# Attention's combine step and the closing output stage of a hybrid decoder layer: longer-lived buffers, two DMA queues, norm weights in PSUM, residual on GpSimd

## The chip, the cores and the metric

The kernel runs on one core of a Trainium2 chip. The core has TensorE (PE, matrix products into PSUM), VectorE (DVE), ScalarE (ACT), GpSimd (POOL) and SyncE (SP, which here only starts DMA transfers), an on-chip memory SBUF and the matrix result memory PSUM with eight banks. Each engine works through its own instruction list strictly in order; a waiting instruction holds up everything behind it on its engine. The metric is the device time of one execution in microseconds (us), less is better: the median of three runs.

## What is computed

One layer of a decoder trunk with four parallel token mixers over 2048 tokens of width 1024, all in float32. What this change touches is the end of mixer A (an attention of four heads of 64 channels, with three dilations whose outputs are weighted by their softmax denominators) and everything behind it:

```
outs, lses = [], []
for window, dil in DILATED_PAIRS:              # three branches
    o, lse = _dilated_branch(q, k, v, window, dil, slopes)
    outs.append(o); lses.append(lse)
w = jax.nn.softmax(jnp.stack(lses), axis=0)    # weights of the branches
ya = jnp.einsum('gbhs,gbhsd->bhsd', w, jnp.stack(outs))
...
y = jnp.concatenate([ya * silu(ag), yb * silu(bg), yc * silu(cg), yd * silu(dg)], axis=-1)
y = jnp.einsum('bse,ed->bsd', y, w_out)        # 1024 x 1024 output projection
return x + _rms_norm(y, post_g)                # residual + normalised projection
```

## The kernel before

**Stages.** The input projection and mixers B, C and D come first (lines 143 to 536); their gated outputs go to memory (`yb_d`). Attention follows in two passes, `attention(0)` for heads 0 and 1 and `attention(1)` for heads 2 and 3. The last stage is the output projection with norm and residual (`final`, line 820), one tile of 128 tokens at a time, 16 tiles. A float32 product is made of three: each operand is split into a rounded "high" part and a "low" remainder, and high*high, high*low and low*high are added up in PSUM. That is why so many places have a copy that makes the high part and a subtraction that makes the low part.

**Order of the work.** The program is written as a dependence graph; a planner, which plays the program on a cost model, fixes each engine's list before anything runs, and earlier program text has priority. The order on each engine is therefore fixed, but the lines of the source do not give it one to one.

**From attention's statistics to the combine.** For each head and dilation `keep_stats` (line 719) writes maxima and denominators to memory (`st_d`). When a head is done, `weigh` (line 737) loads them (line 740, tile `sv`), works out the three branch weights per token on DVE and ACT (lines 741 to 752) and stores them (line 753, `f_d`). `combine` (line 755) then works on a pair of heads, chunk by chunk of tokens: two DMAs (line 763) read the weights of the two heads back, each broadcast over 64 partitions, into `fb` (128 x 3 x chunk); a third (line 765) loads the gate `sga`; POOL multiplies two branches by their weights (lines 766 and 767), DVE the third and adds the three (768 to 770) and applies the gate (772); ACT and DVE or POOL split the result into high and low (776, 777), tile `ysa`. For heads 0 and 1 chunks are 256 tokens with two buffers each for `fb` and `sga`, taken from pool `p2`, and the result goes to memory (`ya_d`, line 779) and comes back for the last stage (tile `ya0`, line 878). For heads 2 and 3 chunks are 512 tokens with two buffers each from pool `p4`, which is opened only after attention's pools `pm` and `p2` are closed, and the result is kept in SBUF. `weigh` and `combine` issue their DMAs on SP. Groups of 512 tokens are taken in the order 2, 3, 0, 1.

**Partials.** For the first 9 token tiles the six non-attention blocks of the projection are done while attention runs: `partial` (line 813) fills PE's gaps, and stores its sum in `part_d` (line 818). `issue_after` ties each partial to a point of the attention. The weights of the output projection are loaded and split by `out_weights` (line 543); blocks 1 to 3 come between the two attention passes, block 0 (the attention channels) after the last partial (line 868).

**The last stage.** Tiles 9 to 15 are "full" (48 matmuls of 128x512 each), tiles 0 to 8 "have" a partial (12 matmuls). `order` starts with the full tiles 9, 10 and 11, then runs three or two have tiles ahead of each full one and ends with full tile 15. A full tile loads its non-attention blocks (`yraw`) and splits them (`split_y`, lines 788 to 800: high part on ACT, low part on DVE). PE sums each 512-wide half in a PSUM bank (tag `fin`, 8 banks). A have tile adds the loaded partial on DVE (836); a full tile is copied by ACT (838). ACT squares and sums (844, for the last tile 840); DVE runs a ten-instruction chain for the inverse root (845, 124 to 135); then DVE multiplies by the root and the norm weights `post_b` (849), adds the residual (850), and SP stores the tile (851). Tile `z4` has 4 buffers, each held from the load of the partial, or from ACT's copy, until the store has landed.

```
for ns in halves if last else [slice(0, DM)]:
    V.scalar_tensor_tensor(z[:, ns], z[:, ns], rstd, post_b[:, ns], ALU.mult, ALU.mult)
    V.tensor_tensor(z[:, ns], z[:, ns], xr[:, ns], ALU.add)
    D.dma_start(out[0, t * P:(t + 1) * P, ns], z[:, ns])
```

Here V is DVE, A is ACT, G is POOL and D is SP.

Of the kernel before, what the change touches and what calls it, by code (L numbers as in the profile page):

```python
# [9 lines left out]
F32 = mybir.dt.float32  # L10
# [4 lines left out]
ALU = mybir.AluOpType  # L15
# [19 lines left out]
SLOPES = tuple(2.0 ** -(2 * (h + 1)) for h in range(4))  # L35
T_1, T_4, T_16, T_HEAD = 0, 256, 512, 640
MASKED = 1e30
PB = {"part": 1, "fin": 8}
N_S, N_T, N_O = 2, 3, 2
CORD = (2, 3, 0, 1)  # L40
CB0, B_PR, B_PT = 2, 6, 3

# [43 lines left out]
def hymba(ctx: ExitStack, tc: tile.TileContext, x, pre_g, w_in, sgu_g, sgu_w, sgu_b, pool_w,  # L86
# [4 lines left out]
    def r32(ap):  # L91
        return ap.bitcast(F32)
# [462 lines left out]
    def attention(p, tab):  # L555
        o01 = (big if p == 0 else po).tile([P, 2, SEQ], F32, tag="big" if p == 0 else "o01", name="att_o01")
        o = [o01[:, 0], o01[:, 1], po.tile([P, SEQ], F32, tag="o2", name="att_o2")]
        for s in range(2):
# [11 lines left out]
            for b, dil in enumerate(DILS):  # L570
# [22 lines left out]
                st = p2.tile([P, 2, 16], F32, tag="stat", bufs=2, name="att_st")  # L593
                branch(h, dil, qb, k2a, k2b, vt, tab, o[b], st)
                keep_stats(h, b, dil, st)
            weigh(h)
        return o

    def branch(h, dil, q2, k2a, k2b, vt, tab, o, st):
# [134 lines left out]
            else:  # L734
                D.dma_start(dst.rearrange("(w r i) -> r w i", r=16, i=8), src.rearrange("r (w i) -> r w i", i=8))

    def weigh(h):

        sv = p2.tile([P, 3, 2, 16], F32, tag="sv", bufs=2, name="sv")
        D.dma_start(sv.rearrange("q b z f -> q (b z) f"), st_d[h].rearrange("b z (q f) -> q (b z) f", f=16))  # L740
# [12 lines left out]
        D.dma_start(f_d[h].rearrange("b (q f) -> q b f", f=16), ew)  # L753

    def combine(p, o, pool, bufs, keep, step, order):

        kept = {}
        nb = step // P
        for c0 in order:
            cs = slice(c0, c0 + step)  # L760
            fb = pool.tile([P, 3, step], F32, tag="fb", bufs=bufs, name="fb")
            for s in range(2):
                D.dma_start(fb[s * HD:(s + 1) * HD], f_d[2 * p + s][:, cs].partition_broadcast(HD))
            sg = pool.tile([P, step], F32, tag="sga", bufs=bufs, name="sga")
            D.dma_start(sg, ag_d[p][:, cs])
            G.tensor_tensor(fb[:, 1], fb[:, 1], o[1][:, cs], ALU.mult)
            G.tensor_tensor(fb[:, 2], fb[:, 2], o[2][:, cs], ALU.mult)
            V.tensor_tensor(fb[:, 0], fb[:, 0], o[0][:, cs], ALU.mult)
            V.tensor_tensor(fb[:, 0], fb[:, 0], fb[:, 1], ALU.add)
# [5 lines left out]
            ys = pool.tile([P, 2, step], F32R, tag="ysa", bufs=4 if keep else CB0, name="ysa")  # L775
            A.activation(ys[:, 0], y, AF.Copy)
            (V if keep else G).tensor_tensor(ys[:, 1], y, r32(ys[:, 0]), ALU.subtract)
            if not keep:
                D.dma_start(ya_d[c0 // GRP][:, :, c0 % GRP:c0 % GRP + step], r32(ys))
            kept[c0 // step] = ys  # L780
        return kept

    def load_y(t, pool):
# [4 lines left out]
    def split_y(raw, pool, eng):  # L788

        ys = []  # L790
        for e in range(0, 6, 3):
            yt = pool.tile([P, 3, 2, P], F32R, tag="yt", bufs=2, name="yt")
            src = raw[:, e:e + 3]
            if eng is A:
                A.activation(yt[:, :, 0], src, AF.Copy)
            else:
                eng.tensor_copy(yt[:, :, 0], src)
            (V if eng is A else G).tensor_tensor(yt[:, :, 1], src, r32(yt[:, :, 0]), ALU.subtract)  # L798
            ys += [yt[:, j] for j in range(3)]
        return ys  # L800

# [11 lines left out]
    def partial(t):  # L813
        z = p3.tile([P, DM], F32, tag="z", bufs=2, name="z")
        ys = split_y(load_y(t, p3), p3, G)
        for n in range(2):
            A.activation(z[:, n * GRP:(n + 1) * GRP], out_proj(ys, range(2, 8), n, ps2, "part"), AF.Copy)
        D.dma_start(part_d[t * P:(t + 1) * P], z)

    def final(t, have, yb, py, p4, ps4, post_b, last):  # L820
# [24 lines left out]
        V.tensor_scalar(ss[:, :1], ss[:, :1], 1.0 / DM, EPS, ALU.mult, ALU.add)  # L845
        rstd = small.tile([P, 16], F32, tag="rstd", name="rstd2")[:, :1]
        rsqrt(rstd, ss[:, :1], 1)
        for ns in halves if last else [slice(0, DM)]:
            V.scalar_tensor_tensor(z[:, ns], z[:, ns], rstd, post_b[:, ns], ALU.mult, ALU.mult)
            V.tensor_tensor(z[:, ns], z[:, ns], xr[:, ns], ALU.add)  # L850
            D.dma_start(out[0, t * P:(t + 1) * P, ns], z[:, ns])
# [19 lines left out]
    ps4 = ctx.enter_context(tc.tile_pool(name="ps4", bufs=8, space=PSUM, reuse_waits="tile"))  # L871
    full, have = list(range(npart, SEQ // P)), list(range(npart))
    early = {t: load_y(t, p3 if i < 2 else p4) for i, t in enumerate(full[:3])}
    post_b = p4.tile([P, DM], F32, name="post_b")
    ya = [[p4.tile([P, 2, GRP], F32R, tag="ya0", bufs=4, name="ya0") for g in range(NG)]]
    ya.append(combine(1, o, p4, 2, True, GRP, [c * GRP for c in CORD]))
    for g in CORD:
        D.dma_start(r32(ya[0][g]), ya_d[g])
# [35 lines left out]
```

## Time and profile before

| what | us |
|---|---|
| median of three runs | 1062.74 (1060.38 to 1069.5) |
| the profiled execution, its own time | 1066.84 |
| span of its instructions | 1065.1 |
| PE busy | 993.5 (93% of the span) |
| DVE busy | 540.4 (51%) |
| ACT busy | 379.6 (36%) |
| POOL busy | 190.9 (18%) |

The profile counts time from the first instruction of the span. A "busy" engine executes an instruction; issuing a DMA does not count. A view of the timeline has start, duration, engine, source line, operation, output and inputs, and in brackets how long the engine had been idle and what it then waited for. The granted clock is TensorE's share of its full speed. The columns of the table by stages are named in its header. Matmuls overlap, so that their starts, and not their durations, tell PE's pace.

### The profile page before, as it was taken

Reading aid. Unit: us, or ns where it says so; the run is one execution under the profiler, and the core shown is the slowest. Engines: PE = TensorE matmul, PEld = TensorE weight load, DVE = VectorE, ACT = ScalarE, POOL = GpSimd, SP = SyncE. Lnnn points to the kernel's source line nnn. Section 1 sums busy time; section 2 is a strip of 40 time slices with the busy share of each in tenths; the row PEclk is TensorE's granted clock in tenths of the full one; section 3 lists DMA queues with packets and bytes.
Section 4 is the critical chain, followed back from the end, with each engine's and each line's share of the span. In section 5 each row is a group of like instructions: output and inputs, shape, how many; then the busy total and the mean of one; then the engine's idle time right before and its main releaser. Section 6 shows DMA issues by size and latency. Waiting matters only on the chain. (4 is left out here: it accounts for less than half of the span.)

```text
span 1065.1 us, 15690 instructions
## 1 busy us (share of the span) xinstructions
PE 993.5 (93%) x5916; PEld 855.0 (80%) x5916; DVE 540.4 (51%) x1547; ACT 379.6 (36%) x851; POOL 190.9 (18%) x195
## 2 busy tenths in 40 slices
PE   5899999999999999999999999979998779988993
PEld 5888898988877988989898787778988569867872
DVE  7611216696332422023763321287776677547898
ACT  6320222131222421122211121498877448513231
POOL 2310012211232000002210134031122351142000
PEclk9999999999999999999999999998999879989997
DMA  8530313233223331042211830395659953484776
GB/s 279 147 99 20 100 60 114 85 120 92 86 79 99 99 100 39 25 135 80 80 41 50 210 119 20 116 213 162 147 168 201 207 152 85 109 270 129 268 259 217
DMA packets 119962, 135.27 MB, mean 127 GB/s; under 512 B 14928, under 2 KB 95952, under 8 KB 117840
## 3 DMA queue, kind: packets, MB, share of 16 engines
q1 hardware_dynamic: 119888, 134.29, 43.6%
q8 instruction: 46, 0.75, 0.3%
q14 instruction: 28, 0.23, 0.1%
HBM read 97.80 MB, written 36.47 MB: 126 GB/s over the span
## 5 line engine op out<-in xcount | busy, mean ns | idle before, releaser
L95 PE MATMUL ps_t<-hh,w 128*128 128x512 f32 x1152 | 370.1, 398 | 2.3 <-DVE b_t L370 2.3
L95 PEld LDWEIGHTS ps_t<-hh,w 128*128 128x128 f32 x1152 | 216.7, 189 | 52.4 <-issue 3.4
L95 PE MATMUL ps_t<-hl,w 128*128 128x512 f32 x576 | 227.6, 395 | 0.0
L95 PE MATMUL ps_m<-w,hh 128*128 128x256 f32 x1024 | 183.8, 282 | 2.0 <-ACT hh L230 1.6
L95 PE MATMUL ps_out<-wo,yt 128*128 128x512 f32 x576 | 155.6, 414 | 6.1 <-DVE yt L798 3.1
L95 PEld LDWEIGHTS ps_m<-w,hh 128*128 128x128 f32 x1024 | 157.5, 190 | 3.9 <-ACT hh L230 2.8
L95 PE MATMUL ps_m<-w,hl 128*128 128x256 f32 x512 | 145.4, 284 | 0.2 <-DVE hl L231 0.2
L95 PEld LDWEIGHTS ps_out<-wo,yt 128*128 128x128 f32 x576 | 109.8, 198 | 31.1 <-DVE yt L798 4.4
L95 PEld LDWEIGHTS ps_t<-hl,w 128*128 128x128 f32 x576 | 108.7, 189 | 24.3 <-issue 1.4
L250 DVE TENSOR_TENSOR w<-raw,w 128x1024 fp32r<-128x1024 f32 x42 | 59.0, 1412 | 109.6 <-ACT w L248 109.4
L95 PEld LDWEIGHTS ps_m<-w,hl 128*128 128x128 f32 x512 | 97.6, 191 | 0.8 <-DVE hl L231 0.4
L641 ACT ACTIVATE att_p<-att_p,att_st 128x128 f32<-128x128 f32 (+1 forms) x192 | 86.4, 453 | 20.5 <-DVE att_st L639 20.0
L248 ACT ACTIVATE w<-raw 128x1024 fp32r<-128x1024 f32 (+1 forms) x56 | 55.0, 997 | 70.1 <-PE ps_t L95 37.6
L639 DVE CUSTOM_DVE_ANT_0 att_p<-ps_s,tab 128x128 f32<-128x128 f32 (+1 forms) x192 | 60.3, 357 | 34.5 <-PE ps_s L95 31.0
L95 PE MATMUL ps_o<-pt_hi,att_v 128*128 128x128 f32 (+1 forms) x204 | 54.4, 287 | 6.2 <-DVE att_o L664 4.2
L649 DVE TENSOR_TENSOR pt_lo<-ps_pt,pt_hi 128x512 fp32r<-128x512 f32 x80 | 51.2, 650 | 12.5 <-ACT pt_hi L648 12.1
L95 PE MATMUL ps_o<-pt_lo,att_v 128*128 128x128 f32 (+1 forms) x204 | 52.8, 294 | 3.5 <-DVE pt_lo L649 3.4
L98 PE MATMUL ps_pt<-ident,att_p 128*128 128x128 f32 x300 | 51.2, 283 | 0.8 <-ACT att_p L641 0.8
L95 PEld LDWEIGHTS ps_o<-pt_hi,att_v 128*128 128x128 f32 x204 | 40.8, 200 | 9.5 <-DVE att_o L664 4.6
L648 ACT ACTIVATE pt_hi<-ps_pt 128x512 fp32r<-128x512 f32 x80 | 44.1, 563 | 11.2 <-PE ps_pt L98 5.7
L95 PE MATMUL ps_s<-k2a,q2b 128*128 128x128 f32 (+1 forms) x128 | 37.5, 325 | 8.6 <-DMA k2a<-qk 4.4
L95 PEld LDWEIGHTS ps_o<-pt_lo,att_v 128*128 128x128 f32 x204 | 40.6, 199 | 5.9 <-DVE pt_lo L649 4.8
(160 smaller groups left out, 1319.8 us busy)
## 6 DMA issues: line engine op xcount, KB each, us to landing
raw<-in_w_in_dram SPq DMA_DIRECT2D x52, 512.0 KB
qk<-qk_s SPq DMA_DIRECT2D x16, 512.0 KB
att_v<-vd SPq DMA_DIRECT2D x8, 1024.0 KB
xr<-in_x_dram SPq DMA_DIRECT2D x16, 512.0 KB
out_dram<-z SPq DMA_DIRECT2D x15, 512.0 KB
xt<-in_x_dram SPq DMA_DIRECT2D x7, 1024.0 KB
yraw<-yb SPq DMA_DIRECT2D x16, 384.0 KB
partd<-z SPq DMA_DIRECT2D x9, 512.0 KB
```

Of the source, the lines that this page charges most:

```text
L95: return T.matmul(o, lhsT, rhs, start=start, stop=stop, skip_group_check=True)
L98: T.transpose(o, i, ident[:n, :n])
L248: A.activation(hi, raw[:, :, cs], AF.Copy, scale=sc)
L250: eng.tensor_tensor(lo, raw[:, :, cs], r32(hi), ALU.subtract)
L639: V.tensor_tensor_reduce(out=pr[:, u, :w], in0=ps[:, u, :w], in1=bb, scale=-SLOPES[h] * HD ** -0.5, scalar=3e38, op0=ALU.add, op1=ALU.min, ...
L641: A.activation(pr[:, u, :w], pr[:, u, :w], AF.Exp, bias=neg, scale=-1.0, accum_out=st[:, 1, n:n + 1])
L648: A.activation(hi, pt[:, :w], AF.Copy)
L649: V.tensor_tensor(lo, pt[:, :w], r32(hi), ALU.subtract)
```

## The change

- `combine` takes `fb` and `sga` from a new pool `pc`, opened ahead of attention's pools and kept to the end. Chunks are 256 tokens for both pairs of heads, two buffers each. The result of heads 2 and 3 is written into tiles of 512 tokens, half by half.
- In `combine` the first head's broadcast and the gate come first, then the second head's broadcast; the latter goes on ACT's DMA queue for heads 2 and 3, as do the load and the store in `weigh` for head 3.
- `post_b` moves to PSUM: the norm weights are loaded into a buffer of tag `z4` and copied by two ACT instructions into a tile of two banks; the banks for projection sums go from 8 to 6.
- Line 849's multiplication is done in halves of 512 for all tiles; the residual (line 850) goes to POOL for all tiles but the last.
- `split_y` makes the low parts on POOL everywhere.
- `out_weights(0)` comes ahead of the last two partials.

```
-PB = {"part": 1, "fin": 8}
+PB = {"part": 1, "fin": 6}
+N_FB = 2
...
-            weigh(h)
+            weigh(h, A if h == 3 else D)
...
-    def weigh(h):
+    def weigh(h, q):
-        D.dma_start(sv..., st_d[h]...)
+        q.dma_start(sv..., st_d[h]...)
-        D.dma_start(f_d[h]..., ew)
-    def combine(p, o, pool, bufs, keep, step, order):
+        q.dma_start(f_d[h]..., ew)
+    def combine(p, o, pool, keep, order):
-        nb = step // P
+        step, nb = 256, 2
+        q = A if keep else D
-            fb = pool.tile([P, 3, step], F32, tag="fb", bufs=bufs, name="fb")
-            for s in range(2):
-                D.dma_start(fb[s * HD:(s + 1) * HD], f_d[2 * p + s][:, cs].partition_broadcast(HD))
-            sg = pool.tile([P, step], F32, tag="sga", bufs=bufs, name="sga")
+            fb = pc.tile([P, 3, step], F32, tag="fb", bufs=N_FB, name="fb")
+            sg = pc.tile([P, step], F32, tag="sga", bufs=N_FB, name="sga")
+            D.dma_start(fb[:HD], f_d[2 * p][:, cs].partition_broadcast(HD))
             D.dma_start(sg, ag_d[p][:, cs])
+            q.dma_start(fb[HD:], f_d[2 * p + 1][:, cs].partition_broadcast(HD))
...
+                    kept[g] = pool.tile([P, 2, GRP], F32R, tag="ysa", bufs=4, name="ysa")
+                ys = kept[g][:, :, part]
...
-            (V if eng is A else G).tensor_tensor(yt[:, :, 1], src, r32(yt[:, :, 0]), ALU.subtract)
+            G.tensor_tensor(yt[:, :, 1], src, r32(yt[:, :, 0]), ALU.subtract)
...
+        for ns in halves:
+            V.scalar_tensor_tensor(z[:, ns], z[:, ns], rstd, post_b[:, ns], ALU.mult, ALU.mult)
         for ns in halves if last else [slice(0, DM)]:
-            V.scalar_tensor_tensor(z[:, ns], z[:, ns], rstd, post_b[:, ns], ALU.mult, ALU.mult)
-            V.tensor_tensor(z[:, ns], z[:, ns], xr[:, ns], ALU.add)
+            (V if last else G).tensor_tensor(z[:, ns], z[:, ns], xr[:, ns], ALU.add)
...
+    pc = ctx.enter_context(tc.tile_pool(name="pc", bufs=1, side="right", reuse_waits="tile"))
...
-        combine(0, o, p2, 2, False, 256, range(0, SEQ, 256))
+        combine(0, o, p2, False, range(0, SEQ, 256))
...
+                if t == npart - 2:
+                    out_weights(0, G)
                 partial(t)
-        out_weights(0, G)
...
-    post_b = p4.tile([P, DM], F32, name="post_b")
+    post_s = p4.tile([P, DM], F32, tag="z4", bufs=4, name="post_s")
+    post_b = ps4.tile([P, DM], F32, tag="gain", bufs=1, name="post_b")
-    ya.append(combine(1, o, p4, 2, True, GRP, [c * GRP for c in CORD]))
+    ya.append(combine(1, o, p4, True, [c * GRP + z for c in CORD for z in (0, 256)]))
-    D.dma_start(post_b, post_g[0].partition_broadcast(P))
+    D.dma_start(post_s, post_g[0].partition_broadcast(P))
+    for n in range(2):
+        A.activation(post_b[:, ns], post_s[:, ns], AF.Copy)      # ns: half n
```

More of the change, by code (lines that the diff above doesn't have):

```diff
@@ L774, in combine @@
                             sg.rearrange("p (n r i) -> p n r i", n=nb, r=16), ALU.mult)
-            ys = pool.tile([P, 2, step], F32R, tag="ysa", bufs=4 if keep else CB0, name="ysa")
+            g, part = c0 // GRP, slice(c0 % GRP, c0 % GRP + step)
+            if keep:
+                if g not in kept:
+                    kept[g] = pool.tile([P, 2, GRP], F32R, tag="ysa", bufs=4, name="ysa")
+                ys = kept[g][:, :, part]
+            else:
+                ys = pool.tile([P, 2, step], F32R, tag="ysa", bufs=CB0, name="ysa")
             A.activation(ys[:, 0], y, AF.Copy)
@@ L778, in combine @@
             if not keep:
-                D.dma_start(ya_d[c0 // GRP][:, :, c0 % GRP:c0 % GRP + step], r32(ys))
-            kept[c0 // step] = ys
+                D.dma_start(ya_d[g][:, :, part], r32(ys))
         return kept
@@ L866, in hymba @@
             with tc.issue_after(marks[int(len(marks) * (t + spread[0]) / npart * spread[1])]):
+                if t == npart - 2:
+                    out_weights(0, G)
                 partial(t)
[L868 removed]
     p4 = ctx.enter_context(tc.tile_pool(name="p4", bufs=1, reuse_waits="tile"))
[L871 removed]
+    ps4 = ctx.enter_context(tc.tile_pool(name="ps4", bufs=6, space=PSUM, reuse_waits="tile"))
     full, have = list(range(npart, SEQ // P)), list(range(npart))
     early = {t: load_y(t, p3 if i < 2 else p4) for i, t in enumerate(full[:3])}
[L874 removed]
+    post_s = p4.tile([P, DM], F32, tag="z4", bufs=4, name="post_s")
+    post_b = ps4.tile([P, DM], F32, tag="gain", bufs=1, name="post_b")
     ya = [[p4.tile([P, 2, GRP], F32R, tag="ya0", bufs=4, name="ya0") for g in range(NG)]]
[L876 removed]
+    ya.append(combine(1, o, p4, True, [c * GRP + z for c in CORD for z in (0, 256)]))
     for g in CORD:
         D.dma_start(r32(ya[0][g]), ya_d[g])
[L879 removed]
+    D.dma_start(post_s, post_g[0].partition_broadcast(P))
+    for n in range(2):
+        ns = slice(n * GRP, (n + 1) * GRP)
+        A.activation(post_b[:, ns], post_s[:, ns], AF.Copy)
     order = full[:3]
```

4 lines of the change are left out of this document (2 added, 2 removed).

## Prediction

> **What bounds the kernel now.** I first read the table by stages (start:end and length of the stretch, then busy us and instruction count of PE, PEld, DVE, ACT and POOL, then PE's granted clock, DMA share, GB/s).
>
> ```profile
> 800.00:880.00 80.00, 64.71 (x354) 54.67 (x353) 54.04 (x166) 42.24 (x136) 30.83 (x37) 0.85 0.81 187
> 880.00:925.00 45.00, 44.80 (x315) 41.19 (x314) 30.77 (x102) 35.38 (x104) 6.07 (x8) 0.99 0.29 67
> 925.00:985.00 60.00, 52.35 (x209) 40.69 (x208) 34.47 (x57) 15.45 (x30) 17.88 (x10) 0.94 0.70 207
> 985.00:1047.00 62.00, 60.28 (x261) 48.49 (x259) 53.79 (x161) 18.06 (x34) 0.00 (x0) 1.00 0.78 268
> 1047.00:1066.00 19.00, 0.00 (x0) 0.00 (x0) 14.72 (x40) 3.56 (x8) 0.00 (x0) 0.61 0.47 171
> ```
>
> Until 925 PE works on attention and partials. From 800 to 880, beside the first combine, it loses 15.3 us idle and a good part of its clock. From 925 on the second combine and the last stage run: PE loses 7.7 us by 985, little until 1047, and then the core runs 18 us without a matmul, with DVE busy nearly throughout. These two losses are where the change works. PE's own timeline, its idle gaps in brackets:
>
> ```profile
> 933.27 0.73 PE L95 MATMUL ps_out<-wo,yt 128*128 128x512 f32 x2 [1.16 <-ACT yt L795]
> 935.70 10.55 PE L95 MATMUL ps_out<-wo,yt 128*128 128x512 f32 x32 [1.71 <-DVE yt L798]
> ...
> 959.77 2.11 PE L95 MATMUL ps_out<-wo,ysa 128*128 128x512 f32 x8 [2.05 <-ACT ysa L776]
> ...
> 977.34 0.51 PE L95 MATMUL ps_out<-wo,ysa 128*128 128x512 f32 x1 [1.48 <-DVE ysa L777]
> ...
> 1041.05 4.28 PE L95 MATMUL ps_out<-wo,yt 128*128 128x512 f32 x18
> 1045.17 0.85 PE L95 MATMUL ps_out<-wo,ya 128*128 128x512 f32 x3
> 1045.85 0.85 PE L95 MATMUL ps_out<-wo,ysa 128*128 128x512 f32 x3
> ```
>
> At full clock 18 matmuls take 1045.17 - 1041.05 = 4.12 us, 0.229 each. The last stage has 7*48 + 9*12 = 444 of them, 101.6 us; begun at 935.7 they could end at 1037.3 and they end at 1046.7. Of the 9.4 us lost, 3.5 are the two waits for ysa; the 32 matmuls at 935.70 lasted 3.2 more than 32 * 0.229. Why ysa is late, and why DVE runs on after PE, stands in the timelines of SP's queue and of DVE:
>
> ```profile
> 928.73 0.37 SPq L753 DMA_DIRECT2D fd<-ew  x1
> ...
> 930.45 4.88 SPq L878 DMA_DIRECT2D ya<-ya  x4
> ...
> 936.23 0.59 SPq L763 DMA_DIRECT2D fb<-fd  x1
> ...
> 985.33 0.34 SPq L851 DMA_DIRECT2D out_dram<-z  x1
> ```
>
> ```profile
> 948.17 0.69 DVE L768 TENSOR_TENSOR fb<-fb,att_o 128x512 f32<-128x512 f32 x1 [12.05 <-DMA fb<-fd]
> ...
> 950.05 1.78 DVE L769 TENSOR_TENSOR fb<-fb 128x512 f32<-128x512 f32 x1 [1.19 <-POOL fb L766]
> ...
> 971.81 0.14 DVE L845 TENSOR_SCALAR ss<-ss 128x1 f32<-128x1 f32 x1
> ...
> 985.94 0.68 DVE L777 TENSOR_TENSOR ysa<-fb,ysa 128x512 fp32r<-128x512 f32 x1
> ...
> 1054.51 0.20 DVE L842 TENSOR_SCALAR ss<-ss 128x1 f32<-128x1 f32 x1
> ...
> 1055.19 1.28 DVE L849 SCALAR_TENSOR_TENSOR z<-z,rstd,post_b 128x1024 f32<-128x1024 f32 x1
> ...
> 1059.32 1.42 DVE L849 SCALAR_TENSOR_TENSOR z<-z,rstd,post_b 128x512 f32<-128x512 f32 x2
> ...
> 1060.65 1.29 DVE L850 TENSOR_TENSOR z<-z,xr 128x512 f32<-128x512 f32 x2
> ```
>
> Head 3's weights leave at 928.73, but SP reaches the broadcast that completes the first chunk only at 936.23, and it lands at 948. DVE stands in front of it for 12 us; the first tile's norm starts only at 971.81, between the later chunks in DVE's order, and the first output leaves at 985.33. From 985.33 to 1060.65 plus a half instruction, 15 further tiles leave at about 5.1 us each. That is DVE's pace, and 54 of 62 us of it are busy. PE gets ahead, and at its end the tiles behind it are still on DVE.
>
> **The change part by part.** The groups by shape, DVE from 985 and POOL from 780:
>
> ```profile
> L850 DVE TENSOR_TENSOR z<-z,xr 128x1024 f32<-128x1024 f32 x15 | 18.3, 1218 | 0.0
> L849 DVE SCALAR_TENSOR_TENSOR z<-z,rstd,post_b 128x1024 f32<-128x1024 f32 x14 | 17.9, 1278 | 0.0
> L798 DVE TENSOR_TENSOR yt<-yraw,yt 128x384 fp32r<-128x384 f32 x6 | 3.3, 550 | 0.1
> L798 POOL TENSOR_TENSOR yt<-yraw,yt 128x384 fp32r<-128x384 f32 x12 | 12.5, 1038 | 0.5
> L767 POOL TENSOR_TENSOR fb<-fb,att_o 128x256 f32<-128x256 f32 x8 | 6.6, 824 | 0.0
> L550 POOL TENSOR_TENSOR wo<-wo_raw,wo 128x1024 fp32r<-128x1024 f32 x2 | 5.2, 2605 | 10.2 <-ACT wo L549 10.2
> ```
>
> *Residual and splits to POOL.* DVE loses 15 * 1.22 = 18.3 us and 14 * 0.55 = 7.7. POOL gains 15 * 2.6 = 39 and 14 * 1.04 = 14.6, 54 us of the 100 in which it is idle now. One tile's residual comes 1.4 us later (2.6 for 1.22), without DVE's queue in front. Halving line 849 makes two of 0.75 for one of 1.28, with overlapping starts: 16 * 0 to 0.22, so 0 to 3.5 us on a DVE that has 26 us given back; I take 1 and hide it there. POOL's instructions slow DVE where both read two SBUF operands: L769 above took 1.78 beside POOL, where 0.69 is usual for 512 (L768). With the norm weights in PSUM line 849 has one SBUF tensor; its nearest relative beside a busy POOL is
>
> ```profile
> 829.75 1.17 POOL L798 TENSOR_TENSOR yt<-yraw,yt 128x384 fp32r<-128x384 f32 x1
> ```
>
> ```profile
> 829.99 0.67 DVE L664 TENSOR_TENSOR att_o<-ps_o,att_o 64x512 f32<-64x512 f32 x1
> ```
>
> 0.67, not slowed. So I cost the PSUM read at nothing; were it slowed as L769 was, 32 halves times 1.1 would be 35 us on DVE and the relief gone. The load of `post_b` moves as it is, and two ACT copies (about 0.6 each, as the ones below) lie in ACT's idle time. Six banks instead of eight hold three tiles; the first three full tiles fill exactly these, so 0, and 2.7 us (one have tile) if PE misses that lead.
>
> POOL's list is in order too: a split of the four later full tiles can stand behind a residual, 0 to 4 * 2.6 us of PE; I take 0, as PE has up to three have tiles (8.2 us) to run meanwhile. A `z4` buffer is held longer. Its store and its load are in the chain of waits:
>
> ```profile
> 990.02 4.75 DMA out_dram<-z
> 994.79 3.44 DMA z<-partd
> ```
>
> With two additions of 0.65, about 1.2 for the square, 2.4 for the inverse root (worked out below), 1.3 for the scaling and 2.6 for the residual, that is 17 us where it was 15.6; four buffers then pass a tile every 4.3 us, and PE needs 101.6 / 16 = 6.3 per tile. So 0, with 0 to 3 us where have tiles come in a row at 2.7 each.
>
> *The end.* After the last matmul at 1046.7 ACT has this to do, and DVE starts the last chain 7.8 us after it, at 1054.51:
>
> ```profile
> 1050.59 0.58 ACT L838 ACTIVATE z<-ps_out 128x512 f32<-128x512 f32 x1
> ...
> 1051.20 0.63 ACT L840 ACTIVATE sq<-z 128x512 bf16<-128x512 f32 x1
> ```
>
> Without a backlog it is 0.58 + 0.63 = 1.2 us: 6.6 less. From 1054.51 to 1059.32 the chain takes 4.8, of which 2.4 are another tile's line 849 (1055.19) and the 850 behind it (1.22 by its group): 2.4 less. Together **-9 us**, if the have tiles ahead are cleared during the last full tile's 11 us of PE; their DVE work is then 2 * 3.6 us. It is 0 if the outputs are as late as now, so -9 to 0.
>
> *Combine.* With `pc` open from the start, the first head's halves and gates of two chunks can be loaded while attention's last head runs (DMA share 0.29 there). What remains after 928.73 is landing of the weights and one broadcast of half the partitions. The chain of waits has such transfers, start and duration:
>
> ```profile
> 799.10 5.85 DMA fd<-ew
> 804.96 5.01 DMA fb<-fd
> ...
> 965.09 9.73 DMA fb<-fd
> ```
>
> So 928.7 + 5.9 + 5.0 to 9.7 gives 940 to 944 in place of 948.2, and a chunk of 256 costs about 5 us to ysa (two POOL instructions of 0.8, six short ones on DVE and ACT) in place of 11.6 (948.2 to 959.8): ysa at 945 to 949, 11 to 15 us earlier. The six later chunks come in pairs, 10 to 15 us per pair: the last at 975 to 994, 986.6 now. PE meets its first ysa about 946 and the group of the have tiles, the second pair behind, near 968. The two waits for ysa go: **-3.5 us** (0 to -3.5). SP loses eight broadcasts of 0.6 and gains the four extra first-head issues and four gate issues; ACT gains ten issues of 0.6, about 6 us, in a stage where it is busy 15 of 60. Where the ACT queue waits, ysa's copies (776), the splits (795) and PSUM copies (838) stand behind it and PE behind these: 0 to 12 us, I take **+1**.
>
> *Output weights ahead.* ACT now waits for these weights in front of tile 9's split:
>
> ```profile
> 931.74 1.06 ACT L549 ACTIVATE wo<-wo_raw 128x1024 fp32r<-128x1024 f32 x1 [3.33 <-DMA wo_raw<-in_w_out_dram]
> ```
>
> PE's gaps of 1.16 and 1.71 follow it, and its 3.2 us at low clock follow these. Moved ahead, up to 6.1 come back; half of it, **-3**, because the split itself goes to POOL at 1.04 for 0.55. The two ACT copies (2.1 us) now fall into attention, where ACT is busy 35 of 45 us and PE all the time: 0 to **+2**, I take 1, PE's partials covering the rest.
>
> *First combine.* It has the same chunks, buffers and queue as before; only the first two chunks' half can be early. I take 0, and 10 us either way, since 800 to 880 holds 15 us of idle PE that a new order can add to or remove.
>
> Sum: -9 - 3.5 + 1 - 3 + 1 = -13.5. The profiled execution would go from 1066.8 to 1053.3; it lies 4.1 above the median shown, so for the median 1062.7 I forecast **1049 us**.
>
> **The rivals.** (1) *The broadcasts stay late.* The same DMA engines carry everything; from 925 to 985 they are busy 70% and SP's four ya issues took 4.88 us. If the half on ACT's queue needs the 12 us that 936.23 to 948.17 shows, ysa comes at about 951, and with 9.7 us per reload plus 5 of work the last is at 995. DVE blocks as now, the tail keeps most of its backlog, and what stays is about 1.1 us per tile at the last four tiles: -4.5, so 1058. For it speaks the saturation, against it that half the bytes come before. The Trainium skill, DMA: Bandwidth & Descriptors, section "Issuing engines are not separate DMA queues", says that starting transfers from several engines saves only issue time because they share the engines; by that rule this rival holds. No row of before shows a transfer on ACT's queue.
>
> (2) *ACT becomes the gate.* ACT's list stops in order at each second-head broadcast: once for the landing of 5.85 us, and up to six times for a buffer that frees only when a chunk's 5 us are done. With half of this hidden that is 5.9 + 15 = 21 us of ACT standing with splits and PSUM copies behind it; PE has six banks to run on. If 60% of it reaches PE, 12.5 us, plus about 5 for the clock that sinks after gaps (0.85 from 800 to 880), less half the tail's gain: +13 and 1076. It decides once PE idles over 21 us from 925 to 985 in place of 7.7. Against it: ACT's low load there.
>
> (3) *The first combine gains too.* DVE stands for a broadcast in attention's path as well. If the early halves remove half of PE's 15.3 us, -8 more: 1041.
>
> **How the numbers follow.** Chances: my forecast 0.50, its own range 1043 to 1056; rival 1 0.27; rival 2 0.13; rival 3 0.10. A change of about 1% (10.6 us) is what a measurement of this kernel can tell from none: faster means under 1052.1, slower over 1073.4. Faster: 0.39 of my 0.50, all of rival 3, 0.03 of rival 1, together 0.52. Slower: 0.10 of rival 2 and 0.01 from a worse first combine, 0.11. Same: 0.37. The range takes in rivals 1 and 3 with the unknown of the first combine, and leaves out most of rival 2: 1036 to 1065.
>
> **What would show it.** Right: the first ysa before 950 and the first output before 970; no PE wait for ysa; DVE under 45 us busy in the last 62 before PE's end; last matmul to end of the span about 10 us in place of 18.4; line 849's halves at about 0.7 beside a busy POOL. Wrong: the last matmul not earlier than now; line 849 over 1 us per half; ACT idle in stretches over 5 us in front of line 776 or 795; PE waiting for POOL's splits; the stretch before 925 longer than now.

## The result and the profile after

The changed kernel takes **1078.91 us** (median, 1076.32 to 1080.11) beside 1062.15 for the kernel before: 1.0127 times as long, interval 1.0094 to 1.0159. It is slower; 1049 was forecast, with 1065 as the upper end. The profiled execution has 1078.01 us as its own time and a span of 1076.2 (before 1066.84 and 1065.1). The medians lie 16.8 us apart and the two profiled spans 11.1, as the kernel before was profiled in an execution above its median; the readings below account for the 11.1.

The table by stages of the changed kernel has the columns of the table of before; the last two stretches together reach to its end:

```profile
800.00:880.00 80.00, 65.57 (x372) 56.02 (x370) 55.26 (x174) 43.21 (x139) 30.58 (x37) 0.87 0.73 186
880.00:925.00 45.00, 39.68 (x272) 36.23 (x271) 27.76 (x92) 34.52 (x101) 10.72 (x10) 0.96 0.37 91
925.00:985.00 60.00, 47.37 (x199) 37.99 (x197) 24.06 (x53) 13.13 (x27) 18.55 (x19) 0.91 0.56 162
985.00:1047.00 62.00, 57.21 (x230) 46.03 (x231) 49.38 (x151) 20.45 (x39) 30.79 (x20) 0.92 0.72 234
1047.00:1078.00 31.00, 14.06 (x62) 11.20 (x60) 19.45 (x63) 5.22 (x12) 14.16 (x8) 0.77 0.62 220
```

The first combine, 800 to 880, is as it was. PE then idles 5.3 us of 45 where it idled 0.2, and 12.6 of 60 where it idled 7.7. Its timeline names the gaps:

```profile
896.87 0.55 PE L96 MATMUL ps_o<-pt_hi,att_v 128*128 128x256 f32 x1 [5.32 <-DVE att_o L665]
...
938.39 6.80 PE L96 MATMUL ps_out<-wo,yt 128*128 128x512 f32 x17 [8.51 <-ACT z L824]
...
986.47 4.21 PE L96 MATMUL ps_out<-wo,ysa 128*128 128x512 f32 x9 [5.59 <-ACT ysa L784]
...
1015.72 5.50 PE L96 MATMUL ps_out<-wo,yt 128*128 128x512 f32 x16 [2.46 <-POOL yt L805]
...
1060.20 0.85 PE L96 MATMUL ps_out<-wo,ysa 128*128 128x512 f32 x3
```

The last matmul ends at 1061.05, 14.4 us later than before. From the tables PE idles 22.7 us between 880 and its last matmul (5.3 + 12.6 + 4.8) where it idled 9.3: 13.4 of the 14.4. From there to the end of the span it is 15.1 us in place of 18.4, a gain of 3.3.

**The first gap** is ACT's, in attention. Its timeline:

```profile
894.33 1.06 ACT L550 ACTIVATE wo<-wo_raw 128x1024 fp32r<-128x1024 f32 x1 [7.72 <-DMA wo_raw<-in_w_out_dram]
895.41 0.59 ACT L664 ACTIVATE att_o<-ps_o 64x512 f32<-64x512 f32 x1
```

The output weights, now ahead of two partials, had not landed, and attention's copies (line 664 and the next line 649) stood behind them.

**The second gap** is again ACT's; its rows, then those of SP's queue (ACTq and SPq mark the issue of a DMA):

```profile
926.80 0.42 ACTq L741 DMA_DIRECT2D sv<-std  x1
...
937.61 0.24 ACT L748 ACTIVATE ew<-df 128x48 f32<-128x48 f32 x1 [8.56 <-DVE df L746]
937.76 0.58 ACT L824 ACTIVATE z<-ps_out 128x512 f32<-128x512 f32 x1
...
939.93 0.37 ACTq L754 DMA_DIRECT2D fd<-ew  x1
...
945.80 0.67 ACTq L767 DMA_DIRECT2D fb<-fd  x1
...
955.62 0.42 ACT L784 ACTIVATE ysa<-fb 128x256 fp32r<-128x256 f32 x1 [7.15 <-DVE fb L774]
```

```profile
925.47 0.85 SPq L792 DMA_DIRECT2D yraw<-yb  x2
926.37 2.15 SPq L889 DMA_DIRECT2D ya<-ya  x4
929.06 0.34 SPq L890 DMA_DIRECT2D post_s<-in_post_g_dram  x1
```

```profile
936.95 0.18 DVE L743 TENSOR_TENSOR nm<-sv 128x16 f32<-128x16 f32 x1 [10.73 <-DMA sv<-std]
```

The last row is DVE's: head 3's statistics, issued on ACT's queue at 926.80, were there only at 936.95, after 10.2 us. In the kernel before SP issued them and DVE began with them after 3.0 us:

```profile
922.49 0.38 SPq L740 DMA_DIRECT2D sv<-std  x1
```

```profile
925.47 0.18 DVE L742 TENSOR_TENSOR nm<-sv 128x16 f32<-128x16 f32 x1 [3.31 <-DMA sv<-std]
```

Meanwhile, in the changed kernel, ACT stood at line 748, and the PSUM copy (824) and the splits for which PE waited stood behind it. SP was free to issue 2.5 MB (four ya loads and post_s, 0.5 MB each) around the load, behind two yraw loads of 0.4 MB. The packet records of the traces show the load in 768 pieces of 64 bytes: here they moved from 930.20 to 936.39, between the pieces of the bulk, in the kernel before from 923.94 to 924.86. The weights leave at 939.93 where they left at 928.73, so the first ysa comes at 955.62; before it was 959.09, the forecast said 945 to 949.

**The end.** The chain of waits of the changed kernel:

```profile
1048.37 2.41 POOL z L858
1050.80 5.75 DMA out_dram<-z
1056.62 4.80 DMA z<-partd
...
1061.61 1.29 DVE z L843 x2
```

It goes through a `z4` buffer: residual, store, load of the next partial into the same buffer, and only then the addition of that partial.

### The profile page after: what moved, and what is told of

The parts are those of the page before. It is cut to its first block, busy times and chain, and to the rows that moved or that the text cites. A ratio compares the mean times of both kernels' runs of the same rounds, so it can differ in the third digit from the quotient of the medians.

```text
span 1076.2 us, 15817 instructions
## 1 busy us (share of the span) xinstructions
PE 994.5 (92%) x5916; PEld 858.8 (80%) x5916; DVE 528.4 (49%) x1553; ACT 382.2 (36%) x857; POOL 240.0 (22%) x232
## 4 chain that ended last, share of the span: by engine, by line
PE 67%; DMA 17%; DVE 8%; issue 4%; POOL 2%; SPq 1%; ACT 1%; DVEq 0%; POOLq 0%; ACTq 0%
PE ps_t L96 37%; PE ps_m L96 15%; DMA fb<-fd 5%; PE ps_out L96 4%; DMA out_dram<-z 2%; PE ps_o L96 2%; PE ps_of L96 2%; DMA wo_raw<-in_w_out_dram 2%; DMA k2b<-qk 2%; PE ps_s L96 2%; PE ps_pt L99 1%; DMA cm<-in_cmix_dram 1%; DMA sv<-std 1%; DMA raw<-in_w_in_dram 1%; PE ps_in L96 1%
## 5 line engine op out<-in xcount | busy, mean ns | idle before, releaser
L642 ACT ACTIVATE att_p<-att_p,att_st 128x128 f32<-128x128 f32 (+1 forms) x192 | 86.4, 453 | 23.0 <-DVE att_st L640 22.7
L445 POOL TENSOR_TENSOR d_g<-d_g,ret_b 128x512 f32<-128x512 f32 x8 | 10.3, 1287 | 181.4 <-ACT d_g L443 181.4
```

Source lines behind the costliest of these rows:

```text
L445: G.tensor_tensor(o, o, ret_b.unsqueeze(1).broadcast_to([P, 2, 256]), ALU.mult)
L642: A.activation(pr[:, u, :w], pr[:, u, :w], AF.Exp, bias=neg, scale=-1.0, accum_out=st[:, 1, n:n + 1])
```

## The experiments

Ratios are to the kernel before in the same batch (its medians were 1061.7 to 1062.8), and it is by ratios that batches are compared.

**Undoing the two placements.** `e1_wo_back` is the changed kernel with block 0 of the output weights back behind the partials, `e2_weigh_sp` with head 3's statistics and weights back on SP, `e3_both` with both.

```
e1, e3:            if t == npart - 2: out_weights(0, G)      removed
                   out_weights(0, G)                         back after the loop
e2, e3: -          weigh(h, A if h == 3 else D)
        +          weigh(h, D)
```

> The changed kernel with the output weights of block 0 loaded after the last partial again, as before the change. If these weights cost time because ScalarE stands 7.7 us in front of their load in the middle of attention (PE waits 5.3 us for it and its clock is 0.91 from 880 to 900), the PE gap at 891 to 897 is gone and the time falls by 5 to 8 us, to about 1072. If that gap was covered by partials anyway and the loss is in the last stage alone, the time stays within 2 us of the changed kernel's 1078.9.

> The changed kernel with head 3's load of statistics and store of weights on SP's queue again; the second head's broadcasts stay on ScalarE's queue. PE, DVE and POOL have the same instruction order as in the changed kernel. If the load took 10.2 us in place of 3.0 because SP went ahead with 2.8 MB of bulk loads while ScalarE was still on its way to the load, the load lands within 4 us now, PE's gap of 8.5 us at 930 shrinks to under 3, and the time falls by 6 to 10 us, to about 1070. If the DMA engines were full in any case and the queue did not matter, the load still takes 8 us or more and the time stays within 2 us of 1078.9.

> The changed kernel with both undone: output weights of block 0 after the partials, head 3's load and store on SP. If the two losses are separate, their gains add up: 12 to 17 us, 1062 to 1067, level with the kernel before. What is then still missing against the forecast of 1049 lies in the serial rounds of broadcasts (PE waits 5.6 us for ysa at 981) and in the tail. If both are the same delay seen twice, the time is that of the better of the two alone, about 1070.

Measured: e1 1068.61 us, 1.0070 (1.0041 to 1.0099); e2 1070.94, 1.0085 (1.0053 to 1.0117); e3 1064.26, 1.0025 (1.0003 to 1.0047). Against the changed kernel's 1.0127 that is 0.6%, 0.4% and 1.0%, so the two placements carry most of the loss (the interval of e3 lies clear of the changed kernel's, those of e1 and e2 overlap it). In e2 PE, DVE and POOL have the same lists as in the changed kernel; its SP and DVE timelines show what the queue did:

```profile
925.98 0.38 SPq L741 DMA_DIRECT2D sv<-std  x1
...
927.00 0.90 SPq L889 DMA_DIRECT2D ya<-ya  x2
```

```profile
929.10 0.18 DVE L743 TENSOR_TENSOR nm<-sv 128x16 f32<-128x16 f32 x1 [3.55 <-DMA sv<-std]
```

3.1 us, with two ya loads only 1.0 us behind it on the same queue; PE's gap there is 1.34 us. The gap in attention stays (4.44). In e1 the gap in attention is gone and the one for the statistics is 1.80 us: SP has a `wo_raw` load ahead of ya again, ya is issued 3.1 us after the statistics, and these take 3.9 us although they are on ACT's queue. So the place of the output weights also decides when ya comes: the two placements are not independent, although their gains add up (0.6 and 0.4%).

**Each placement alone, on the kernel before.** `e10_weigh_act` puts head 3's statistics and weights on ACT's queue, `e11_wo_first` the output weights ahead of the last two partials, `e13_weigh_act_wo_first` does both. The combine is that of before in all three.

```
e10, e13: -  weigh(h)
          +  weigh(h, A if h == 3 else D)
e11, e13: +  if t == npart - 2: out_weights(0, G)     (and the call after the loop removed)
```

> The kernel before with one part alone: head 3's load of statistics and store of weights on ScalarE's queue. PE, DVE and POOL keep their order. If the load loses its place in front of SP's bulk loads, it takes 6 us or more from issue to use in place of 3.0 and the last stage starts later: 4 to 9 us more, 1066 to 1071. If the changed kernel's loss came from other work at that time, the load still lands within 4 us and the time stays within 2 us of 1062.

> The kernel before with one part alone: output weights of block 0 ahead of the last two partials. If ScalarE then stands in front of their load within attention, as in the changed kernel, there is a PE gap of 4 us or more between 880 and 900 and the time rises by 3 to 8 us, to 1065 to 1070, less what the earlier weights save behind attention (PE's gaps of 1.16 and 1.71 us at 932 and 935). If the forecast's step was right, it falls by 2 to 4 us.

> The kernel before with two of the changed kernel's steps, head 3's load and store on ACT's queue and block 0 of the output weights ahead of the last two partials; the combine is as before. Theory (each step is harmless while SP's queue still stops at head 3's broadcast, which waits for its weights and so keeps the ya loads back): sv lands in 3 to 5 us, ACT waits under 4 us in attention for the output weights, time as with the output weights alone, 1058 to 1062. Rival (the two steps together are enough for the loss, the combine has no part in it): sv over 8 us, time 1066 to 1074.

Measured: e10 1062.46 us, 1.0004 (0.9984 to 1.0024); e11 1059.02, 0.9976 (0.9956 to 0.9995); e13 1065.21, 1.0018 (1.0001 to 1.0036). Alone the queue costs nothing and the output weights gain; together they lose 0.4% against e11, though PE, DVE and POOL have the same lists as there. ACT and SP of e10, then of e13:

```profile
919.86 0.41 ACTq L740 DMA_DIRECT2D sv<-std  x1
...
925.57 0.24 ACT L747 ACTIVATE ew<-df 128x48 f32<-128x48 f32 x1 [3.18 <-DVE df L745]
```

```profile
922.26 0.34 SPq L548 DMA_DIRECT2D wo_raw<-in_w_out_dram  x1
...
925.79 4.77 SPq L878 DMA_DIRECT2D ya<-ya  x4
```

```profile
922.01 0.42 ACTq L740 DMA_DIRECT2D sv<-std  x1
...
932.55 0.24 ACT L747 ACTIVATE ew<-df 128x48 f32<-128x48 f32 x1 [7.99 <-DVE df L745]
```

```profile
920.50 0.63 SPq L763 DMA_DIRECT2D fb<-fd  x1
...
922.49 0.60 SPq L765 DMA_DIRECT2D sga<-agd  x1
923.13 0.68 SPq L879 DMA_DIRECT2D ya<-ya  x1
...
931.88 0.80 SPq L879 DMA_DIRECT2D ya<-ya  x2
```

In e10 SP stands before the `wo_raw` load until 922.26; the broadcasts of head 2 go out from 923.17, ya 5.9 us after the statistics, and these take 4.3 us (DVE begins at 924.18). In e13 no `wo_raw` load is left on SP at this place. Two broadcasts and two gate loads (1.3 MB) go out from 920.50, ahead of the statistics and beside them, and one ya load 1.1 us behind; the statistics take 9.9 us (931.89), and PE waits 8.88 us, as in the changed kernel. The next two ya loads leave only at 931.88: SP itself stood for the statistics, 8.1 us. So here the bulk beside the load is mostly that of head 2's broadcasts and gates. The theory that SP's queue would hold ya back in e13 behind head 3's broadcast has fallen: SP's list has three of the ya loads ahead of it. The new combine isn't needed for this wait; of its 8.9 us about half shows in the time (0.4%).

**The bulk loads behind the statistics.** `e15_ya_act` is the changed kernel with the ya and post_s loads on ACT's queue.

```
-        D.dma_start(r32(ya[0][g]), ya_d[g])
-    D.dma_start(post_s, ...)
+        A.dma_start(r32(ya[0][g]), ya_d[g])
+    A.dma_start(post_s, ...)
```

> The changed kernel with the four loads of ya and the load of post_s on ACT's queue, where they stand behind head 3's load of sv instead of running ahead on SP. Theory (bulk loads that SP is free to issue overtake sv): sv lands 3 to 6 us after its issue in place of 10.2, ACT's wait in front of the weights falls from 8.6 to under 5 us and PE's gap of 8.5 us at 938 to under 5; but two of the ya loads now stand ahead of the store of the weights on ACT's own queue, so the weights land later and the time gains only part of the 8 us that undoing the queue gave: 1072 to 1078. Rival (a load on ACT's queue is slow whatever SP issues): sv still takes about 10 us, the gap at 938 stays over 7, time as the changed kernel or more, 1078 to 1082.

Measured: 1075.58 us, 1.0119 (1.0074 to 1.0163), not to be told from the changed kernel by the time. DVE's timeline shows the mechanism:

```profile
932.96 0.18 DVE L743 TENSOR_TENSOR nm<-sv 128x16 f32<-128x16 f32 x1 [4.66 <-DMA sv<-std]
...
946.60 1.87 DVE L770 TENSOR_TENSOR fb<-fb,att_o 128x256 f32<-128x256 f32 x2 [11.10 <-DMA fb<-fd]
```

The statistics, issued at 928.89, take 4.1 us on the same queue of ACT on which they took 10.2; ya follows 4.8 us after them, and PE's gap falls from 8.5 to 2.4 us. So it is not ACT's queue that is slow; the bulk of another queue overtakes. SP does issue three loads of x (1.5 MB) from 930.54 on, 1.7 us behind the statistics; by the packet records the pieces of the statistics had all moved by 932.43, so this bulk came too late to matter. The time doesn't follow: two of the ya loads stand ahead of the store of the weights (issued at 935.53), their broadcast is there only at 946.60, and ysa and a split on POOL then hold PE for 3.7 and 3.3 us. The gap in attention stays too (3.55).

**Only the norm, and one buffer more.** `e4_norm_alone` is the kernel before with the norm weights in PSUM, six banks, line 849 in halves, and residual and low parts on POOL. `e5_z5` has five `z4` buffers in addition: the norm weights took 4 KB of each partition in SBUF, and a `z4` buffer is as large. `e8_resid_dve` is e4 with the residual left on DVE, `e12_z5_resid_dve` e8 with five buffers.

```
e4: the diff of the change at PB, split_y, final, ps4 and post_b alone
e5, e12: -  z = p4.tile([P, DM], F32, tag="z4", bufs=4, name="z4")
         +  z = p4.tile([P, DM], F32, tag="z4", bufs=5, name="z4")
e8, e12: -  (V if last else G).tensor_tensor(z[:, ns], z[:, ns], xr[:, ns], ALU.add)
         +  V.tensor_tensor(z[:, ns], z[:, ns], xr[:, ns], ALU.add)
```

> The kernel before with only the last stage's part of the change: norm weights in PSUM with six banks for sums, line 849 in halves, residual and low parts of the split on GpSimd. If this part is what makes the changed kernel slow (residual twice as long, split behind it, buffers of z held longer), the time is over 1070. If it is the part that gives the shorter tail, DVE is under 45 us busy from 985 to 1047 and the time falls by 3 to 9 us, to 1053 to 1059. If z's buffers set the pace of outputs and not DVE, DVE falls idle on loads of partials and the time stays within 3 us of 1062.

> The kernel before with the last stage's part alone, as in the run of that part, and five buffers of z instead of four. In that run DVE's idle time in front of line 836 was mostly for loads of partials (4.4 and 4.8 us at 1023 and 1037), which wait for a store to free a buffer of z. If these buffers set the pace behind PE, the last store comes 3 to 6 us earlier and the time is 1054 to 1057. If the end hangs on PE's last matmul and the last tile's own chain, five buffers change less than 2 us (1059.6).

> The kernel before with the last stage's part, but the residual left on DVE: norm weights in PSUM, halves, low parts of the split on GpSimd. If the relief of DVE by the residual gives the 2.4 us that the part gained, the time is back at 1062. If the residual on GpSimd costs as much in holding z (2.4 us against 1.2) as it relieves DVE, the time is the same, 1058 to 1061.

> The kernel before with norm weights in PSUM, low parts of the split on GpSimd and five buffers of z, the residual on DVE. If the number of z buffers is what gave the gain from 1059.6 to 1055.2, and the residual on GpSimd only lengthens each buffer's hold, the time is 1053 to 1056. If DVE's load becomes the pace as soon as the buffers no longer are, it is 1058 to 1061, and the residual on GpSimd is worth its place only with five buffers.

Measured: e4 1059.64 us, 0.9960 (0.9932 to 0.9988); e5 1055.16, 0.9922 (0.9898 to 0.9946); e8 1059.99, 0.9977 (0.9955 to 0.9999); e12 **1052.83**, 0.9919 (0.9892 to 0.9947). The last stretches of e4, then of e12, and between them e4's DVE:

```profile
985.00:1047.00 62.00, 59.20 (x258) 47.94 (x256) 44.62 (x156) 20.31 (x41) 32.29 (x17) 1.00 0.77 263
1047.00:1078.00 31.00, 0.00 (x0) 0.00 (x0) 7.45 (x23) 0.41 (x2) 4.68 (x2) 0.79 0.16 63
```

```profile
1022.88 0.69 DVE L836 TENSOR_TENSOR z<-ps_out,z 128x512 f32<-128x512 f32 x1 [4.39 <-DMA z<-partd]
...
1036.51 0.69 DVE L836 TENSOR_TENSOR z<-ps_out,z 128x512 f32<-128x512 f32 x1 [4.81 <-DMA z<-partd]
```

```profile
985.00:1047.00 62.00, 51.48 (x225) 41.93 (x224) 56.67 (x166) 18.27 (x34) 6.33 (x6) 0.95 0.76 268
1047.00:1078.00 31.00, 0.00 (x0) 0.00 (x0) 0.00 (x0) 0.00 (x0) 0.00 (x0) 0.94 0.00 2
```

In e4 DVE is relieved as forecast, 44.6 us busy where it was 53.8, yet it stands for 9.2 us in front of these two partials, which wait for a buffer. In e12 DVE keeps the residual. Its 56.7 us run to the very end of that kernel, while the kernel before has 14.7 us more behind its 53.8. What sets the end is read from the chains of waits, here of e4, then of e5:

```profile
1032.02 5.61 DMA out_dram<-z
1037.65 4.64 DMA z<-partd
```

```profile
984.82 58.34 PE ps_out L95 x250
```

With four buffers the chain passes through a store and the load of a partial into the freed buffer, in e4 as in the changed kernel (and in e8, 4.65 and 3.76 us). With five no load of a partial is left in it: in e5 it follows PE to the last matmul, and then come only the last tile's own 9.75 us; in e12, with the residual on DVE, it is DVE's from 1015.73 on but for one store of 3.0 us, with 12.1 us behind the last matmul. So with four buffers the buffers set the end, and with five PE (e5) or DVE (e12). In the time the place of the residual makes no difference that the intervals show, with four buffers or with five; the fifth buffer makes 0.4% (intervals that still meet) on e4 and 0.6% on e8.

**The combine.** On e3, `e7_bcast_sp` puts the second head's broadcasts on SP, `e6_five_bufs` gives the six later chunks three more pairs of `fb` and `sga` from `p4`, and `e9_four_bufs_z5` two more pairs and five `z4` buffers.

```
e7: -  q = A if keep else D
    +  q = D
e6: +  src, nbuf = (pool, 3) if keep and i >= N_FB else (pc, N_FB)     (e9: 2 for 3, z4 bufs=5)
    +  fb = src.tile([P, 3, step], F32, tag="fb", bufs=nbuf, name="fb")     (sg likewise)
```

> The run with both undone, with the second head's broadcasts on SP's queue as well, so that nothing is issued on ScalarE's queue. If the own queue is what brings the second head's half early (7.5 us from issue to use, ahead of SP's bulk loads), the first ysa comes 3 to 8 us later than 945.9 and the time rises by 2 to 5 us. If the queues share the same DMA engines and only issue time is saved, the time stays within 2 us of 1064; if ScalarE's in-order waits cost more than they save, it falls by 1 to 4 us.

> The run with both undone (output weights after the partials, head 3's statistics on SP), with three further buffers for the six later chunks of the second combine, from the last stage's pool: five chunks under way instead of two. If four rounds of broadcast and combine, about 12 us each, are what keeps ysa late, the chunk rounds overlap, PE's waits for ysa (11.6 us together) fall under 5, and the time falls by 5 to 9 us, to 1055 to 1059. If the DMA engines' bandwidth sets the rounds, ysa comes no earlier and the time stays within 2 us of 1064.

> The changed kernel with output weights after the partials and head 3's statistics on SP, two further buffers for the six later chunks, and five buffers of z. If z's buffers were what kept the freed rounds of the run with five chunk buffers from showing in the time, the time falls under that of the last stage's part with five z, to 1049 to 1055. If the combine by 256 tokens brings nothing of its own, it is 1055 to 1059; if its extra instructions cost, over 1059.

Measured: e7 1068.16 us, 1.0053 (1.0033 to 1.0073); e6 1063.41, 1.0004 (0.9979 to 1.0028); e9 1061.57, 0.9996 (0.9980 to 1.0012). By e7 the own queue is worth about 0.3%, though its interval meets that of e3; the first chunk's multiplication on DVE starts at 941.20 there, in e3 at 938.72. In e3 the chunks come in rounds, as each needs a buffer that an earlier one frees (DVE's timeline, first multiplication of the first, third and last chunk):

```profile
938.72 0.99 DVE L770 TENSOR_TENSOR fb<-fb,att_o 128x256 f32<-128x256 f32 x1 [16.13 <-DMA fb<-fd]
...
955.09 0.43 DVE L770 TENSOR_TENSOR fb<-fb,att_o 128x256 f32<-128x256 f32 x1 [5.56 <-DMA fb<-fd]
...
997.75 0.43 DVE L770 TENSOR_TENSOR fb<-fb,att_o 128x256 f32<-128x256 f32 x1 [3.69 <-DMA fb<-fd]
```

The first chunk is there 9.4 us earlier than in the kernel before (948.17), as forecast, but the last only at 997.75. PE waits for ysa at three places (2.1, 2.2 and 7.3 us), and 4.3 us more for a PSUM copy: ACT had stood 6.3 us in front of a chunk's ysa, and the copy stood behind it. With more buffers, in e6, no wait for ysa over 0.8 us is left, and other waits are: 2.8 us for a split on ACT, 2.5 for the output weights, 3.2 for a split on POOL. Neither e6 nor e9 differs from the kernel before. e3 is e4 (0.9960) with the new combine, e9 has the five buffers of e5 (0.9922), and both are slower than these by more than their intervals; e6 against e4 points the same way, with intervals that overlap. So the new combine as a whole returns nothing here and costs what the norm part gains. By these ratios the 1.27% of the changed kernel are made up of -0.4% for the norm part (e4), +0.65% for the combine (e3 against e4) and +1.0% for the two placements (the changed kernel against e3).

**The best parts together.** `e14_z5_wo_first` is e12 with the output weights ahead, as in e11.

> The best version so far (norm weights in PSUM, line 849 in halves, residual on DVE, five z4 buffers, combine as before) with block 0 of the output weights ahead of the last two partials. Theory (the gain of 2.7 us that this step brought alone on the kernel before lies at 925 to 946, ahead of the outputs, so it adds to the gain of the fifth buffer): 1049 to 1051, ratio 0.989. Rival (the outputs at the end set the time, so an earlier start of the last stage is lost again in front of the norms): 1052 to 1054; and if the new list lets ACT wait in attention for these weights as in the changed kernel, PE idles over 3 us before 900 and the time is 1056 or more.

Measured: 1055.07 us, 0.9928 (0.9900 to 0.9955): the gain of e11 doesn't add. PE waits 3.97 us for ysa at 949.49, and its last matmul ends at 1040.5 where e12's ended at 1036.5. The list of PE is another one from attention on, so that these two kernels differ in more than the step. e12, e5 and e14 aren't told apart by their intervals; each beats both kernels of this study.

## Why the prediction was wrong

- **Combine, "ysa at 945 to 949" and ACT "+1".** This step failed. It took head 3's weights as leaving at 928.73, as before: it counted the load and the store among ten issues on ACT's queue and had no term for the load's own time. For waits on ACT's queue it allowed 0 to 12 us and took 1. The weights left at 939.93, 11.2 us late: the load was issued 4.3 us later, behind the gap in attention, and took 10.2 us in place of 3.0. ACT stood 8.6 us in front of its result, PE 8.5. What follows came as priced: 5.9 us for the weights to land (939.93 to 945.80), 5.5 for the broadcast (to 951.27), 4.3 to ysa. The trigger is not on ACT: SP was free to run ahead into the bulk loads (e13 has the same wait with the old combine, e15 and e1 lose it when the bulk comes later). The first output left at 986.31, where before 970 was forecast.
- **Output weights ahead, "-3" and "+1".** Right alone: e11 gains 0.24%, 2.7 us, and the gap at 935.70 is gone there. In the changed kernel ACT stood 7.7 us for these weights, PE 5.3. The text bounded the cost in attention at 2 us, the ACT copies' own time; a wait ahead of the copies was not in the bound. In e11 the same copy waits 2.35 us and no gap of PE follows. That the early broadcasts, which SP issues just ahead at 879.71 and 881.43, make the difference fits the traces, but no kernel separates it.
- **The first pair early, "-3.5".** The size of the first chunk was right once the placements are undone (938.7 in e3; 940 to 944 forecast for the landing), and so was that the later pairs depend on a buffer. The gain of PE's waits was wrong: 11.6 us of waits for ysa in e3, 3.5 before. "10 to 15 us per pair" was written down, but "the last at 975 to 994" was taken as harmless. Also, SP doesn't lose eight broadcasts: before there were eight in all (four chunks, two heads), and eight stay on SP.
- **The end, "-9 to 0".** It was sized by DVE's backlog. DVE's relief came (44.6 in e4, and 47.1 in the last 62 us before the changed kernel's last matmul, where under 45 was forecast) and the end shrank by 3.3 us in the changed kernel, 5.2 in e4 and 8.7 in e5 (9.75 us from the last matmul to the end, where about 10 was forecast). What stood between was the reuse of `z4`, which the prediction put at "4.3 us per tile" against 6.3 for PE and so at 0, with 0 to 3 us for partial tiles in a row. This term was too small: each partial needs its buffer a store and a load ahead (5.75 and 4.80 us in the changed kernel, 4.75 and 3.44 in the sum), and DVE stands 11.1 us for partials from 985 on. In e5, with the fifth buffer, the end is the one that was forecast.
- **Norm weights in PSUM, 0.** Right. The group of the halves in the changed kernel, beside a POOL busy with the residual of 2.41 us:

```profile
L858 POOL TENSOR_TENSOR z<-z,xr 128x1024 f32<-128x1024 f32 x15 | 36.1, 2414 | 26.0 <-ACT z L845 11.6 <-DVE rs_t L135 7.1 <-issue 5.7
...
L856 DVE SCALAR_TENSOR_TENSOR z<-z,rstd,post_b 128x512 f32<-128x512 f32 x32 | 22.5, 743 | 0.4
```

- **The first combine, 0.** Right: PE idles 14.4 us from 800 to 880, before 15.3.
- **The rivals.** Rival 2, ACT as the gate at 1076, had chance 0.13 and comes nearest, with the right mechanism (PE behind an ACT that stands in order) and the wrong place: in the changed kernel the long waits are for the statistics and the output weights. In e3, with both placements undone, ACT does stand in the combine and PE behind it (4.3 us for the PSUM copy), but in front of a ysa copy and not of a broadcast. Its condition, PE idle over 21 us from 925 to 985, didn't occur: 12.6 there, the rest lies ahead of 900 and behind 985. Rival 1 weighed the rule of the Trainium skill (DMA: Bandwidth & Descriptors, "Issuing engines are not separate DMA queues") that transfers from several engines share what carries them for the broadcasts alone. The 10.2 us of the statistics agree with that rule. The broadcasts were not late by it: 5.5 us on ACT's queue in the changed kernel and 7.5 in e3, where the forecast had 5.0 to 9.7 and the rival 12. The "four ya issues" of 4.88 us, which the rival took for saturation, are four issues of 0.32 to 0.43 us; between them SP waited for other transfers.

## What to carry to other kernels

When a small load that others wait for is moved to another queue, look at what its old queue will issue in the freed place: the position ahead of the bulk was the protection, and it is lost without any instruction getting slower. Price each load on a computing engine's queue with the wait of everything behind its consumer on that engine, not with its issue. And size a relief at the end by the resource that releases the next tile, here a buffer through a store and a load, before the busiest engine is taken for it.

## What the runs showed of the hardware that was not expected

- **Queues and bulk.** The same load of 48 KB took 10.2 us in the changed kernel, 3.1 us with ya 1.0 us behind it on its own queue (e2), 9.9 with broadcasts, gates and one ya load on another queue, from 1.5 us ahead of it to 1.1 us behind (e13), and 4.3 and 4.1 where only yraw loads (0.4 and 0.8 MB) were beside it and further bulk followed 2.4 and 1.7 us later (`wo_raw` in e10, x in e15). The Trainium skill, DMA: Bandwidth & Descriptors, section "Queues, rings and completion order", says that descriptors of one ring are consumed in order; the 3.1 us agrees. It also says that an engine goes round between its rings packet by packet. The packet records show the load's 768 pieces of 64 bytes within 1.4 us in e2, 2.2 in e10 and 1.4 in e15, but spread over 5.4 us in e13 and 6.2 in the changed kernel, and begun 3.8 and 3.4 us after the issue in place of 1.4 to 2.2. They don't name the DMA engine, so that the turns of the two queues are not shown.
- **DVE beside POOL.** In e3 a DVE multiplication of two SBUF operands that takes 0.43 us elsewhere lasted as long as the POOL residual beside it; DVE's row, then POOL's:

```profile
968.54 2.53 DVE L770 TENSOR_TENSOR fb<-fb,att_o 128x256 f32<-128x256 f32 x1
```

```profile
968.20 2.59 POOL L858 TENSOR_TENSOR z<-z,xr 128x1024 f32<-128x1024 f32 x1
```

The halves of line 856, with one operand in PSUM, stayed at 736 to 750 ns in the changed kernel.
